# A 2x2 average pool on one Trainium2 core: one vector reduction per tile in place of two adds, and one store for two tiles

## Chip, cores, metric

One core of one Trainium2 chip. The metric is device time in microseconds (us) of the whole kernel. Executions of the kernel before agree within 0.02%. Each experiment ran together with the kernel before on one chip; where two experiments are compared with each other, the kernel before is the link, and its medians in all sets of runs lie between 3104.07 and 3104.31 us.

Names of the profile: DVE is VectorE, ACT is ScalarE, SP is the engine that issues the loads, ACTq and SPq are the sequencers that issue DMAs, L55 is line 55 of that kernel. "Span" is the time from the first to the last instruction of the profiled run, about 2 us under the device time.

## The reference

```python
# x: float32 [32, 128, 256, 256], kernel_size 2, stride 2
output[:, :, i, j] = np.mean(x[:, :, 2*i:2*i+2, 2*j:2*j+2], axis=(2, 3))
```

1073.74 MB are read and 268.44 MB written; three additions and a multiplication make one output.

## The kernel before

Two input rows of one plane (2 x 256 values, adjacent in memory) make one output row of 128. Such units are dealt out in tiles of 32 units for each of the 128 partitions: 64 KB of input and 16 KB of output per partition. There are 127 whole tiles; the last 32 units are loaded in parts of 16, 8, 4 and 4, so that little work is left after the last load.

```python
TILE = 32
in_pool  = tile_pool(bufs=2)      # 2 x 64 KB per partition
out_pool = tile_pool(bufs=4)      # 4 x 16 KB per partition

def pool(it, dst):
    nc.vector.tensor_add(out=it[:, :, 0:w], in0=it[:, :, 0:w], in1=it[:, :, w:])   # L54: the two rows
    nc.vector.tensor_add(out=dst, in0=it[:, :, 0:w:2], in1=it[:, :, 1:w:2])        # L55: the two columns
    nc.scalar.mul(out=dst, in_=dst, mul=0.25)                                      # L56

for k in range(whole):                          # 127 tiles
    it, res = tiles()
    nc.sync.dma_start(out=it, in_=xt)           # load
    pool(it, res)
    if k < whole - 1:
        nc.scalar.dma_start(out=ot, in_=res)    # store, 2 MB
    else:
        held = (ot, res)                        # its store is issued after the last loads
# ... the parts of the last 32 units are loaded; then the held store; then for each part:
    pool(it[:, a:b], res[:, a:b])
    nc.scalar.dma_start(out=ot, in_=res[:, a:b])
```

With two input buffers, the load of tile k+2 can be issued only when VectorE has finished with tile k.

## Time and profile before

| | before |
|---|---|
| device time, median | 3104.2 us (3104.09 to 3104.42) |
| DMA rate over the span | 433 GB/s |
| mean time from one tile's load landing to the next one's, in mid-run | 24.20 us |
| VectorE per whole tile | 8.69 + 4.43 us |

From the page of the kernel before: the instructions and shares of the engines, the DMA packets, the two DMA queues (q1 carries the loads, q10 the stores; the last number is the time that their packets took, as a share of 16 DMA engines over the span), the chain that ended last, and the DMA issues (how many, KB each where the page has it, median us from issue to landing).

```profile
span 3102.3 us, 1081 instructions
...
DVE 1679.7 (54%) x262; ACT 464.8 (15%) x132; POOL 0.2 (0%) x4
...
DMA packets 37736, 1342.26 MB, mean 433 GB/s; under 512 B 4192, under 2 KB 4192, under 8 KB 4576
...
q1 hardware_dynamic: 19008, 1075.85, 80.1%
q10 hardware_dynamic: 18720, 266.35, 20.1%
...
DMA 72%; DVE 27%; issue 0%; DVEq 0%; ACT 0%; SPq 0%
...
out_dram<-res ACTq DMA_DIRECT2D x126, 2048.0 KB, 31.6
...
in_tile<-in_x_dram SPq DMA_DIRECT2D x127, 35.1
```

The groups of instructions, forms apart, of the kernel before. After the bar: busy us in all, mean ns of one | idle time of the engine just before them, and what ended it.

```profile
L54 DVE TENSOR_TENSOR in_tile<-in_tile 128x8192 f32<-128x8192 f32 x127 | 1103.9, 8692 | 1402.8 <-DMA in_tile<-in_x_dram 1402.8
L55 DVE TENSOR_TENSOR res<-in_tile 128x4096 f32<-128x4096 f32 x127 | 562.1, 4426 | 11.7 <-DVE in_tile L54 0.5
```

The two queues add up to 100% of the 16 engines' time. That is the limit of this kernel: in the packet records a 64 KB packet of a load takes 2.418 us and a 16 KB packet of a store 0.611 us (medians), and a tile has 8 of each on every engine. VectorE idles 1402.8 us before the row adds of the whole tiles, every time for a load. The 27% of VectorE in the chain is no cost by itself: the chain follows one buffer at a time (load, adds, next load into that buffer), while the other buffer's load keeps the engines busy. A load takes 35.1 us from issue to landing, where the period is 24.2 us, because it is issued 10.9 us before the load ahead of it lands and queues behind that one. This time is called the lead below. While the DMA engines set the pace, it is about the period less VectorE's time on a tile: 24.2 - 13.2 us here.

The end of the kernel before, from its timeline (start us, us, engine, line, operation, [idle before <- what ended it]):

```profile
3067.22 8.69 DVE L54 TENSOR_TENSOR in_tile<-in_tile 128x8192 f32<-128x8192 f32 x1 [10.96 <-DMA in_tile<-in_x_dram]
3076.00 4.42 DVE L55 TENSOR_TENSOR res<-in_tile 128x4096 f32<-128x4096 f32 x1
...
3081.76 4.42 DVE L54 TENSOR_TENSOR in_tile<-in_tile 128x4096 f32<-128x4096 f32 x1 [1.34 <-DMA in_tile<-in_x_dram]
...
3086.28 2.29 DVE L55 TENSOR_TENSOR res<-in_tile 128x2048 f32<-128x2048 f32 x1
...
3093.81 1.22 DVE L54 TENSOR_TENSOR in_tile<-in_tile 128x1024 f32<-128x1024 f32 x1
...
3095.06 0.69 DVE L55 TENSOR_TENSOR res<-in_tile 128x512 f32<-128x512 f32 x1
...
3096.45 0.34 ACTq L94 DMA_DIRECT2D out_dram<-res  x1
```

The last whole tile's load lands at 3067.2 us. VectorE then works almost without a break on that tile and on the four parts until 3095.75 us, and the last small store lands 4.9 us after its issue.

### The profile page before, as it was taken

To read this page: it belongs to the slowest core of one execution; us is meant where nothing else is said; L and a number is where in the kernel's file an instruction comes from. 1 tells how busy PE (TensorE), PEld (TensorE's weight loads), DVE (VectorE), ACT (ScalarE), POOL (GpSimd) and SP (SyncE) were. 2 spreads that over 40 slices of the span, in tenths; PEclk is the share of its full clock that TensorE was granted. 3 is DMA by queue.
4 is the path that set the end of the run, shared out by engine and by line. 5 is a ranking of instruction groups with operands and counts; after the bars stand their busy time and mean duration, and the time that the engine had idled before them with its cause. 6 is when DMAs were issued, how large, how long until landed. Compare 5 with 4: busy or idle time off the path is not lost.

```text
span 3102.3 us, 1081 instructions
## 1 busy us (share of the span) xinstructions
DVE 1679.7 (54%) x262; ACT 464.8 (15%) x132; POOL 0.2 (0%) x4
## 2 busy tenths in 40 slices
DVE  4555555555555555555555555555555555555556
ACT  1111111111111111111111111111111111111111
POOL 0000000000000000000000000000000000000000
DMA  9999999999999999999999999999999999999999
GB/s 418 437 439 425 437 439 424 438 438 425 438 437 425 439 436 426 439 434 428 440 433 429 439 432 431 438 431 433 437 428 437 437 428 436 437 428 436 437 428 410
DMA packets 37736, 1342.26 MB, mean 433 GB/s; under 512 B 4192, under 2 KB 4192, under 8 KB 4576
## 3 DMA queue, kind: packets, MB, share of 16 engines
q1 hardware_dynamic: 19008, 1075.85, 80.1%
q10 hardware_dynamic: 18720, 266.35, 20.1%
q14 instruction: 8, 0.07, 0.0%
HBM read 1073.74 MB, written 268.44 MB: 433 GB/s over the span
## 4 chain that ended last, share of the span: by engine, by line
DMA 72%; DVE 27%; issue 0%; DVEq 0%; ACT 0%; SPq 0%
DMA in_tile<-in_x_dram 72%; DVE in_tile L54 18%; DVE res L55 9%; DVEq L55 0%; ACT res L56 0%; SPq L74 0%
## 5 line engine op out<-in xcount | busy, mean ns | idle before, releaser
L54 DVE TENSOR_TENSOR in_tile<-in_tile 128x8192 f32<-128x8192 f32 (+1 forms) x131 | 1113.0, 8496 | 1404.2 <-DMA in_tile<-in_x_dram 1404.2
L56 ACT ACTIVATE res<-res 128x4096 f32<-128x4096 f32 (+1 forms) x131 | 463.5, 3538 | 2630.9 <-DVE res L55 2630.9
L55 DVE TENSOR_TENSOR res<-in_tile 128x4096 f32<-128x4096 f32 (+1 forms) x131 | 567.0, 4328 | 11.8 <-DVE in_tile L54 0.5
L56 ACT ACT_TABLE_LOAD x1 | 1.3, 1283 | 0.7 <-PEq L171 0.7
L171 POOL MEMSET const-bfloat16-1.0<- 128x1 bf16 x1 | 0.1, 102 | 0.0
L171 POOL MEMSET const-uint8-127<- 128x1 uint8 x1 | 0.1, 101 | 0.0
L171 POOL MEMSET const-float32-0.0<- 128x1 f32 x1 | 0.1, 99 | 0.2 <-issue 0.2
L171 POOL MEMSET const-float32-1.0<- 128x1 f32 x1 | 0.1, 98 | 0.0
## 6 DMA issues: line engine op xcount, KB each, us to landing
out_dram<-res ACTq DMA_DIRECT2D x126, 2048.0 KB, 31.6
in_tile<-in_x_dram SPq DMA_DIRECT2D x1, 4096.0 KB, 25.5
in_tile<-in_x_dram SPq DMA_DIRECT2D x1, 2048.0 KB, 30.0
in_tile<-in_x_dram SPq DMA_DIRECT2D x2, 1024.0 KB, 33.0
out_dram<-res SPq DMA_DIRECT2D x1, 2048.0 KB, 13.6
in_tile<-in_x_dram SPq DMA_DIRECT2D x127, 35.1
out_dram<-res ACTq DMA_DIRECT2D x1, 1024.0 KB, 8.3
out_dram<-res ACTq DMA_DIRECT2D x1, 512.0 KB, 6.1
```

Source lines behind the costliest of these rows:

```text
L54: nc.vector.tensor_add(out=it[:, :, 0:w], in0=it[:, :, 0:w], in1=it[:, :, w:])
L55: nc.vector.tensor_add(out=dst, in0=it[:, :, 0:w:2], in1=it[:, :, 1:w:2])
L56: nc.scalar.mul(out=dst, in_=dst, mul=0.25)
L171: nc = _bacc.Bacc("TRN2", target_bir_lowering=False, num_devices=1)
```

## The change

The intent: one VectorE instruction per tile instead of two, and half as many stores, each twice as large. A `tensor_reduce` over the axes XY of a rearranged view sums the four values of an output. Two tiles share one output buffer of 2 x 16 KB per partition and one store of 4 MB; there are two such buffers, so four tiles fit as before, but their room comes free by pairs. The diff is shortened: the old loop and the new view `ot` of the output are left out.

```diff
-    out_pool = ctx.enter_context(tc.tile_pool(name="outp", bufs=4))
+    out_pool = ctx.enter_context(tc.tile_pool(name="outp", bufs=2))
-    def pool(it, dst):
-        nc.vector.tensor_add(out=it[:, :, 0:w], in0=it[:, :, 0:w], in1=it[:, :, w:])
-        nc.vector.tensor_add(out=dst, in0=it[:, :, 0:w:2], in1=it[:, :, 1:w:2])
-        nc.scalar.mul(out=dst, in_=dst, mul=0.25)
+    def sums(it, dst):
+        win = it.rearrange("p g (a j b) -> p g j a b", a=2, b=2)
+        nc.vector.tensor_reduce(out=dst, in_=win, axis=mybir.AxisListType.XY, op=mybir.AluOpType.add)
 # ... in the loop over whole tiles
+        if k % 2 == 0:
+            res = out_pool.tile([P, 2, TILE, w_out], f32, name="res")
+        sums(it, res[:, k % 2])
+        nc.scalar.mul(out=res[:, k % 2], in_=res[:, k % 2], mul=0.25)
+        if k % 2 == 1 or k == whole - 1:
+            n = k % 2 + 1
+            store = ot[:, k + 1 - n:k + 1], res[:, 0:n].rearrange("p t g f -> p t (g f)")
+            if k < whole - 1:
+                nc.scalar.dma_start(out=store[0], in_=store[1])
 # ... the last 32 units
+    last = out_pool.tile([P, 2, TILE, w_out], f32, name="res")
+    for to, a, b in parts:
+        dst = last[:, 0, a:b]
+        sums(it[:, a:b], dst)
+        nc.scalar.mul(out=dst, in_=dst, mul=0.25)
+        nc.scalar.dma_start(out=to, in_=dst)
```

More of the change, by code (lines that the diff above doesn't have):

```diff
@@ L61, in block @@
         return xt, ov[rows].rearrange("(p g) f -> p g f", p=P)
-    def tiles():
-        it = in_pool.tile([P, TILE, 2 * w], f32, name="in_tile")
-        return it, out_pool.tile([P, TILE, w_out], f32, name="res")
     whole, rest = divmod(units - 1, TILE)
     rest += 1
+    ot = ov[0:whole * TILE * P].rearrange("(t p g) f -> p t (g f)", p=P, g=TILE)
     for k in range(whole):
-        xt, ot = block(k * TILE * P, TILE)
-        it, res = tiles()
-        nc.sync.dma_start(out=it, in_=xt)
-        pool(it, res)
-        if k < whole - 1:
-            nc.scalar.dma_start(out=ot, in_=res)
-        else:
-            held = (ot, res)
-    it, res = tiles()
+        it = in_pool.tile([P, TILE, 2 * w], f32, name="in_tile")
+        nc.sync.dma_start(out=it, in_=block(k * TILE * P, TILE)[0])
+        if k % 2 == 0:
[7 more added lines that the diff above has]
+                nc.scalar.dma_start(out=store[0], in_=store[1])
+    it = in_pool.tile([P, TILE, 2 * w], f32, name="in_tile")
+    last = out_pool.tile([P, 2, TILE, w_out], f32, name="res")
     parts, a = [], 0
@@ L86, in _pool_2x2 @@
         b = rest if rest - a <= 4 else a + (rest - a) // 2
-        xt, ot = block((whole * TILE + a) * P, b - a)
+        xt, to = block((whole * TILE + a) * P, b - a)
         nc.sync.dma_start(out=it[:, a:b], in_=xt)
-        parts.append((ot, a, b))
+        parts.append((to, a, b))
         a = b
-    nc.sync.dma_start(out=held[0], in_=held[1])
-    for ot, a, b in parts:
-        pool(it[:, a:b], res[:, a:b])
-        nc.scalar.dma_start(out=ot, in_=res[:, a:b])
+    nc.sync.dma_start(out=store[0], in_=store[1])
+    for to, a, b in parts:
[3 more added lines that the diff above has]
+        nc.scalar.dma_start(out=to, in_=dst)
 def _generic_pool(ctx, tc, x, out, k, s, n, c, h, w, h_out, w_out):
```

## The prediction

> **What bounds the kernel now.** The 16 DMA engines. The queue table gives the loads 80.1% and the stores 20.1% of 16 engines' span: nothing is left. In the packet records a 64 KB load packet takes 2.418 us and a 16 KB store packet 0.611 us (medians), both about 27 GB/s per engine. The Trainium skill ("DMA: Bandwidth & Descriptors", Specifications) puts the ceiling of the 16 engines at 435 GB/s; the page of this trace has 433. A tile period is 24.2 us (8 load packets and 8 store packets per engine, 8 x 3.03 us). VectorE is 54% busy: per tile 8.69 us (rows) and 4.43 us (columns), then 11 us waiting for the load (waits view). The chain of waits reads DMA 72%, DVE 27%, but DVE there costs nothing: a load takes 35.1 us from issue to landing against a period of 24.2 us, so while VectorE frees one buffer the other load keeps the engines busy.
>
> **What the change does.** No byte is saved. Two adds (13.1 us, 12288 outputs per partition) become one reduction that reads 16384. The adds fit (elements + about 150) / 0.96 ns; the Trainium skill ("VectorE: DVE Perf Modes", The perf-mode tier table) gives tensor_reduce only 1x, one element per cycle. Estimate: 16384 elements at the traced slope of 1.04 ns = 17.2 us per tile. No trace shows a reduction yet. VectorE then goes from 54% to about 71% busy: 4 us more per tile, off the critical path while busy time plus waiting stays under 24.2 us. 126 stores become 63 of 4 MB with the same packets.
>
> **New wait.** The output buffer holds four tiles as before, but comes free by pairs. If the queues alternate packet by packet, as a store's 31.6 us for 8 packets suggests (8 x 3.03 = 24.2 us, plus the rest of the store before it), a pair's 16 packets need 48.4 us and land about 55 us after issue. Issued 20.8 us after the second tile's load, it lands some 76 us after that; the next tile to need the buffer arrives after three periods (72.6 us). So VectorE should wait about 3 to 4 us for the store at every second tile, 200 us in total, inside its slack (17.2 + 3.6 < 24.2).
>
> **Where it shows in the time.** Only at the end. After the last full tile's load VectorE needs 13.1 + 15.3 us now; then 17.2 + 17.7 us, plus several us waiting until the pair before frees the third buffer. About 15 us are added there, of which some 5 to 7 come back because deferred stores let that load land earlier. Net +8 us (estimate).
>
> **Prediction: 3112 us, range 3103 to 3130. Faster by over 2%: 0.01; within 2%: 0.91; slower by over 2%: 0.08.**
>
> **What would show it.** Right: a reduction near 17.2 us; VectorE about 70% busy; queue shares still adding to 99 to 100%, about 432 GB/s; a wait of VectorE for the store of res, 3 to 4 us at every second tile; pair store about 55 us to landing, loads about 30; the last full load landing earlier than 3067 us, but the end later. Wrong step by step: reduction of 22 us or more (windows of four cost extra cycles); no wait for the store (queues don't alternate as I think).
>
> **What would make it wrong.** The reduction costing extra per window or per jump between rows: above about 23.5 us it sets the period, and each further us per tile costs 128 us (26 us: about 3350). Pair stores whose packets are split unevenly over the engines, or starving the loads.

## The result and the profile after

The median went from 3104.31 to 3110.51 us (3110.2 to 3110.88, 4 runs of each). The ratio is 1.002, 95% interval 1.0005 to 1.0035. Ratios are the mean time of one kernel's fast runs over that of the other's of the same rounds, so not quite the ratio of the medians quoted.

From the page of the changed kernel, the lines that answer to those above:

```profile
span 3108.4 us, 824 instructions
...
DVE 2204.3 (71%) x131; ACT 464.8 (15%) x132; POOL 0.2 (0%) x4
...
DMA packets 36727, 1342.25 MB, mean 432 GB/s; under 512 B 3184, under 2 KB 3184, under 8 KB 3568
...
q1 hardware_dynamic: 19008, 1075.85, 79.9%
q10 hardware_dynamic: 17712, 266.34, 20.0%
...
DMA 64%; DVE 35%; DVEq 0%; ACT 0%; issue 0%; SPq 0%
...
out_dram<-res ACTq DMA_DIRECT2D x63, 4096.0 KB, 51.6
...
in_tile<-in_x_dram SPq DMA_DIRECT2D x127, 31.0
```

Its groups of instructions, forms apart:

```profile
L55 DVE TENSOR_REDUCE res<-in_tile 128x4096 f32<-128x16384 f32 x127 | 2186.9, 17220 | 893.4 <-DMA in_tile<-in_x_dram 885.0 <-DMA out_dram<-res 8.4
...
L55 DVE TENSOR_REDUCE res<-in_tile 128x2048 f32<-128x8192 f32 x1 | 8.7, 8686 | 7.1 <-DMA out_dram<-res 7.1
```

Both kernels over the same stretch of mid-run, 1000 to 2000 us (busy time of the engines, granted clock, share of the DMA engines, GB/s); first the kernel before, then the changed one:

```profile
1000.00:2000.00 1000.00, 537.83 (x82) 151.07 (x42) 0.00 (x0) 1.00 1.00 433
```
```profile
1000.00:2000.00 1000.00, 707.75 (x43) 151.88 (x42) 0.00 (x0) 1.00 1.00 434
```

In mid-run nothing was lost: VectorE has 170 us more to do in 1000 us, the DMA engines are at 1.00 in both, and the period is 24.18 us against 24.20. What is new is at the end. The timeline of the changed kernel there:

```profile
3063.12 17.22 DVE L55 TENSOR_REDUCE res<-in_tile 128x4096 f32<-128x16384 f32 x1 [7.24 <-DMA in_tile<-in_x_dram]
...
3087.43 17.40 DVE L55 TENSOR_REDUCE res<-in_tile 128x2048 f32<-128x8192 f32 x4 [7.09 <-DMA out_dram<-res]
...
3105.52 0.34 ACTq L95 DMA_DIRECT2D out_dram<-res  x1
```

The account from this timeline and the one shown of before, in us:

| | before | after | difference |
|---|---|---|---|
| VectorE starts on the last whole tile | 3067.22 | 3063.12 | -4.1 |
| VectorE on that tile (to 3080.42; 3080.34) | 13.20 | 17.22 | +4.0 |
| wait until the first part can start | 1.34 | 7.09 | +5.8 |
| the four parts | 13.99 | 17.40 | +3.4 |
| from there to the end of the span | 6.55 | 3.59 | -3.0 |
| span | 3102.3 | 3108.4 | +6.1 |

The last whole tile's load lands earlier because some store traffic has been put off behind it: with the pair store alone (e2 below) it lands at 3062.0 us, with the reduction alone (e1) at 3067.0. The wait of 7.09 us is for the pair store of tiles 124 and 125, whose buffer the parts need. The last stores no longer queue behind others: the very last lands 2.0 us after issue, before it was 4.9 us.

### The profile page after: what moved, and what is told of

The parts are those of the page before. It is cut to its first block, busy times and chain, and to the rows that moved or that the text cites. A ratio compares the mean times of both kernels' runs of the same rounds, so it can differ in the third digit from the quotient of the medians.

```text
span 3108.4 us, 824 instructions
## 1 busy us (share of the span) xinstructions
DVE 2204.3 (71%) x131; ACT 464.8 (15%) x132; POOL 0.2 (0%) x4
## 4 chain that ended last, share of the span: by engine, by line
DMA 64%; DVE 35%; DVEq 0%; ACT 0%; issue 0%; SPq 0%
DMA in_tile<-in_x_dram 63%; DVE res L55 35%; DMA out_dram<-res 1%; DVEq L186 0%; ACT res L72 0%; ACT res L94 0%; SPq L68 0%; DVEq L55 0%
## 5 line engine op out<-in xcount | busy, mean ns | idle before, releaser
L55 DVE TENSOR_REDUCE res<-in_tile 128x4096 f32<-128x16384 f32 (+1 forms) x131 | 2204.3, 16829 | 900.5 <-DMA in_tile<-in_x_dram 885.0
L72 ACT ACTIVATE res<-res 128x4096 f32<-128x4096 f32 x127 | 459.2, 3616 | 2622.7 <-DVE res L55 2622.7
## 6 DMA issues: line engine op xcount, KB each, us to landing
out_dram<-res ACTq DMA_DIRECT2D x63, 4096.0 KB, 51.6
```

Source lines behind the costliest of these rows:

```text
L55: nc.vector.tensor_reduce(out=dst, in_=win, axis=mybir.AxisListType.XY, op=mybir.AluOpType.add)
L72: nc.scalar.mul(out=res[:, k % 2], in_=res[:, k % 2], mul=0.25)
```

## Experiments

The theory: mid-run is bound by the DMA engines and does not change; the +6 us are made after the last whole tile's load, by a slower VectorE and by the wait for a pair store. Rivals: the reduction slows the DMA stream; or the pair store makes the whole cost. Twelve kernels ran, all with correct results.

### Each half alone

e1_reduce_only is the kernel before with the reduction:

```diff
-        nc.vector.tensor_add(out=it[:, :, 0:w], in0=it[:, :, 0:w], in1=it[:, :, w:])
-        nc.vector.tensor_add(out=dst, in0=it[:, :, 0:w:2], in1=it[:, :, 1:w:2])
+        win = it.rearrange("p g (a j b) -> p g j a b", a=2, b=2)
+        nc.vector.tensor_reduce(out=dst, in_=win, axis=mybir.AxisListType.XY, op=mybir.AluOpType.add)
```

> Edit: the kernel before with its two adds replaced by the one reduction; stores stay single, four output buffers. Theory (all of the cost lies after the last full tile's load; in mid-run the DMA engines set the pace): the last full load lands where it did in the kernel before (3067 us of the span), then VectorE needs 17.2 + 17.4 us in place of 13.1 + 15.3, ends about 6 us later, and about 3 us come back because the last small stores no longer queue behind others: time +3 us on the kernel before, so 3106 to 3109, no wait of VectorE for a store. Rival A (the pair store makes the whole cost): 3104 to 3105. Rival B (the reduction slows the DMA stream in mid-run, e.g. by SBUF contention): the mean period of a tile rises over 24.20 us and the whole +6 us shows here.

Measured: 3107.36 us (3107.01 to 3108.84) against 3104.07 us of before (3103.98 to 3104.43); ratio 1.0011, interval 0.9999 to 1.0024. The difference of 3.3 us is small against the interval of the ratio, but the ranges of the runs don't touch. Mean period in mid-run 24.18 us, so rival B falls. The last whole tile's load lands at 3067.0 us as before, VectorE works from there on without a break and ends at 3101.6 us, 5.8 us later than before, and never waits for a store:

```profile
3067.04 34.53 DVE L55 TENSOR_REDUCE res<-in_tile 128x4096 f32<-128x16384 f32 x5 [6.96 <-DMA in_tile<-in_x_dram]
```

e2_pair_only is the changed kernel with the two adds:

```diff
-        win = it.rearrange("p g (a j b) -> p g j a b", a=2, b=2)
-        nc.vector.tensor_reduce(out=dst, in_=win, axis=mybir.AxisListType.XY, op=mybir.AluOpType.add)
+        nc.vector.tensor_add(out=it[:, :, 0:w], in0=it[:, :, 0:w], in1=it[:, :, w:])
+        nc.vector.tensor_add(out=dst, in0=it[:, :, 0:w:2], in1=it[:, :, 1:w:2])
```

> Edit: the changed kernel with the two adds put back; pair stores stay. Theory: the last full load lands near 3063 us (stores are put off), VectorE ends that tile at 3076, then waits for the pair store of tiles 124 and 125 to free the third buffer until about 3083 to 3085, then 13.5 us of parts and 3 to 4 us of last store: 3101 to 3104 of span, so time 3102 to 3106, about 0 to +2 on the kernel before, with one wait of VectorE for a store of 7 to 9 us at the end. Rival A (pair store makes the cost): 3110.

Measured: 3104.10 us (3103.89 to 3104.48), ratio 1.0, interval 0.9987 to 1.0014. Rival A falls: the pair store alone costs nothing. The wait at the end is there, but 2.9 us long and not 7 to 9, because the row add of the first part needs no output buffer and runs while the store is still landing (waits from 3000 us to the end):

```profile
DVE res L55 <- DMA out_dram<-res: 2.9, 1, 2.9
```

The halves alone give +3.3 and 0.0 us, both together +6.2. So about 2.9 us come only from the two together: with the reduction the first part's only instruction needs the buffer at once.

### The wait at the end

e3_free_half takes the wait away from the changed kernel. Tile 126 has no partner, so half of its output buffer is unused, and the parts go there:

```diff
-    last = out_pool.tile([P, 2, TILE, w_out], f32, name="res")
-        dst = last[:, 0, a:b]
+        dst = res[:, 1, a:b]
```

> Edit: the changed kernel, but the last small parts are written into the unused second half of tile 126's output buffer, so that they wait for no earlier store. Theory: the last wait of 7 us goes; parts run at once after tile 126 (3080 us), the last ends near 3098, span about 3101 to 3103, time 3103 to 3106: 5 to 7 us below the changed kernel. Rival C (the last wait is slack, since the last loads land only at 3092 and DMA work ends when it ends): unchanged, 3110.

Measured: 3105.29 us (3104.54 to 3105.83), 5.2 us under the 3110.51 us of the changed kernel. The waits of the changed kernel, then of this one, from 3000 us to the end (who waited for whom: us in total, times, longest):

```profile
DVE res L55 <- DMA in_tile<-in_x_dram: 27.8, 4, 7.2
...
DVE res L55 <- DMA out_dram<-res: 7.1, 1, 7.1
```
```profile
DVE res L55 <- DMA in_tile<-in_x_dram: 27.9, 4, 7.2
ACT res L94 <- DVE res L55: 10.1, 4, 5.0
```

The second list has no wait for out_dram. So the 7.1 us wait was on the path, and rival C falls. The rest of the +6 us, about 1 us, is what the slower VectorE still costs: e4 below, which differs from this run in the two adds alone, is 1.3 us faster.

e4_adds_free_half has the two adds, pair stores and the free half together (the edits of the last two runs).

> Edit: the pair-store kernel with the two adds (as in the run before the last) and the last parts in the free half. Theory: VectorE done with each part about 2 us after its load lands (3092), span 3098 to 3101, time 3100 to 3103, one to four us below the kernel before: the most that this schedule can give, since the DMA engines are then busy nearly to the end. Rival: no better than the kernel before, 3104.

Measured: 3103.97 us (3103.94 to 3104.07), ratio 1.0. My expectation of 3100 to 3103 was missed, and the rival holds. VectorE does end a little earlier, at 3094.6 us, but the last load lands at 3092.6 us and the put-off stores are still in the queue, so that the last store takes 6.1 us to land. With the bytes given, no version of these parts beats the kernel before by anything that the runs can tell.

### Does a store wait for the one before it?

I had predicted a wait of VectorE for a store at every second tile, 200 us in all. The changed kernel has two waits that a store ended in the whole run: 8.4 us at the fifth tile, of which only the last 0.8 us are the store's (that tile's load had landed by then), and 7.1 us at the end. A pair store took 51.6 us to land, not 55, and landed 0.18 us before the load of the tile that needs its buffer (the median from the sixth pair on; the least is 0.18 too). I thought that 55 us failed because the backlog of stores, which I had read off the kernel before, is made once at the start. e5_single_two tests it with single stores in two output buffers:

```diff
 # e1_reduce_only, and
-    out_pool = ctx.enter_context(tc.tile_pool(name="outp", bufs=4))
+    out_pool = ctx.enter_context(tc.tile_pool(name="outp", bufs=2))
```

> Edit: single stores and the one reduction, with two output buffers of one tile in place of four. A store is issued 20.8 us after its tile's load landed, and the buffer is needed again 48.4 us after that landing, so only 27.6 us are there for a store; in the kernel before a store took 31.6 us. View 1 (the step of the prediction that failed: the queue keeps a standing backlog from store to store): VectorE waits about 4 us for a store at every tile, some 500 us in all, still hidden (17.2 + 4 < 24.2), time 3107 to 3111. View 2 (the backlog is made at the start only, where the first two loads land 19.3 us apart while a store takes 24.2 us, and a wait drains it for good): one to three waits at the start, under 15 us in all, stores then land in 27.2 to 27.6 us, time 3107 to 3111 as well. The waits view tells the two apart, not the time.

Measured: 3186.40 us (3177.23 to 3197.19), ratio 1.0276, interval 1.0247 to 1.0306. Neither view had this: both expected at most 3111 us. The waits of this run:

```profile
DVE res L55 <- DMA out_dram<-res: 942.7, 125, 13.9
DVE res L55 <- DMA in_tile<-in_x_dram: 24.8, 2, 22.7
```

VectorE waits 7.5 us in the mean for a store, at 125 of 127 tiles. The time closes over one buffer: a store is issued 20.9 us after VectorE starts on its tile and lands 28.5 us later, 49.4 us for two tiles, 24.7 us each. So a wait at every tile (view 1), but not hidden. At the same time packets became longer: with the engines busy all the time, a load's packet took 2.481 us in the mean of mid-run, not 2.418, and 8 of them with 8 of a store (0.611 us) fill 24.7 us as well. Which of the two comes first, the late store or the long packets, this run can't tell. The long packets were new, and the next runs meet them again.

### How much slack does VectorE have?

The prediction held that VectorE is free up to the period of 24.2 us. e6_pad4 and e7_pad9 add work to the changed kernel that nobody needs, and that holds the input buffer longer:

```diff
         sums(it, res[:, k % 2])
+        nc.vector.tensor_add(out=it[:, 0:16, 0:w], in0=it[:, 0:16, 0:w], in1=it[:, 0:16, w:])   # e6: 4.4 us
+        nc.vector.tensor_add(out=it[:, :, 0:w], in0=it[:, :, 0:w], in1=it[:, :, w:])            # e7 instead: 8.7 us
```

> Edit: the changed kernel plus one add of 4096 outputs (4.4 us) on the input tile after every full tile's reduction: work that nobody needs, which holds the input buffer 4.4 us longer. VectorE 21.7 us per tile. Theory (slack of 24.2 us per tile): mean period of a tile stays 24.18 us within 0.05; at the end the extra 4.4 us falls into the 7 us wait for the pair store, so the time stays 3109 to 3113. Rival (VectorE time costs in mid-run, its 35% of the chain of waits being real): a part of 127 x 4.4 = 560 us shows, at least 3160.

Measured: 3353.86 us (3353.42 to 3354.91), ratio 1.0805. My theory falls. The rival's range holds, but its reason does not survive e9 and e10 below: they add 127 x 2.3 and 127 x 1.2 us to VectorE and cost 8.0 and 1.3 us. Mid-run of this run and its DMA queues, to be held against those above:

```profile
q1 hardware_dynamic: 19008, 1075.85, 75.1%
q10 hardware_dynamic: 17712, 266.34, 20.1%
```
```profile
1000.00:2000.00 1000.00, 827.08 (x79) 141.08 (x39) 0.00 (x0) 1.00 0.95 400
```
```profile
1506.86 17.22 DVE L55 TENSOR_REDUCE res<-in_tile 128x4096 f32<-128x16384 f32 x1 [8.98 <-DMA in_tile<-in_x_dram]
...
1524.11 4.42 DVE L72 TENSOR_TENSOR in_tile<-in_tile 128x4096 f32<-128x4096 f32 x1
1527.76 0.38 ACTq L78 DMA_DIRECT2D out_dram<-res  x1
1528.46 17.21 DVE L55 TENSOR_REDUCE res<-in_tile 128x4096 f32<-128x16384 f32 x1
...
1545.70 4.42 DVE L72 TENSOR_TENSOR in_tile<-in_tile 128x4096 f32<-128x4096 f32 x1
1559.16 17.22 DVE L55 TENSOR_REDUCE res<-in_tile 128x4096 f32<-128x16384 f32 x1 [9.04 <-DMA in_tile<-in_x_dram]
```

VectorE takes two tiles without a break, then idles 9.0 us: 52.3 us for two tiles. The DMA engines are at 0.95 here. The packet records show why. The load queue runs dry at 1526.4 us, because VectorE frees the next buffer only at 1528.5 us. That load is issued 0.8 us after a pair store. Its first packet starts 5.0 us after its issue, and until then the pair store has the engines to itself, 7 of its 16 packets per engine. The stores are then over early, the other load of the pair runs without stores in 19.7 us, and the queue runs dry again. The rhythm repeats to the end: landings are 32.3 and 19.9 us apart in turn.

> Edit: the same with an add of 8192 outputs (8.7 us). VectorE 25.96 us per tile with its gaps, over the 24.2 us that the DMA engines need. Theory: VectorE now sets the period, 25.96 us; 22.95 + 127 x 25.96 = 3320 us at the end of the last full tile, then 17.4 us of parts and about 6 us: 3335 to 3350, VectorE 99% busy, about 402 GB/s. If the slack were less than I think, more; if the DMA engines could give way, less.

Measured: 3397.52 us (3396.45 to 3398.44), ratio 1.0945. VectorE is 97% busy and all but sets the period, but the time is 48 us above my range: VectorE waits 0.9 to 1.0 us at every second tile, 62 us in all, as a late load takes 26.9 us to land. So of the 287 us that 8.7 us per tile cost (against 3110.51), 243 had come with the first 4.4 us.

### Is it the start, the lead or the pair?

e8_pad4_late adds the 4.4 us only from the ninth tile on, when the regular rhythm stands:

```diff
         sums(it, res[:, k % 2])
+        if k >= 8:
+            nc.vector.tensor_add(out=it[:, 0:16, 0:w], in0=it[:, 0:16, 0:w], in1=it[:, 0:16, w:])
```

> Asked because the run with 4.4 us more per tile took 250 us more, where I had expected none. Edit: the same extra add of 4.4 us, but only from the ninth tile on, so that the start is that of the changed kernel. View S (the start decides: while no store was in flight a load took 19.3 us, VectorE's 21.7 us let the load queue run dry, and the bad rhythm then repeats; once stores are queued without a gap a load takes 24.2 us and 21.7 us fit): 3110 to 3116. View L (lead decides: in the changed kernel a load is issued 6.9 us before the one ahead of it lands; with 4.4 us less, and a load that is issued just after a pair store giving its first packet only 5 us later, the load queue runs dry at once, stores go alone, and the later load runs without stores at 19.3 us): 3340 to 3356, land-to-land times alternating near 32 and 20 us.

Measured: 3334.97 us (3332.70 to 3337.02), ratio 1.0743. The range of view L began 5 us higher, but view S is out by 219 us: the good rhythm holds for two tiles after the work is added, and then it falls into the bad one (32.3 and 19.9 us). The first gap shows how: load 10 is issued when the load ahead has 1.2 us of packets left, and its first packet starts 3.6 us after the issue. The last pair store had been issued 25.3 us earlier and was still landing.

e9_pad2 and e10_pad1 add 2.3 and 1.2 us (`it[:, 0:8, ...]` and `it[:, 0:4, ...]` in the line of e6).

> Edit: the changed kernel plus an add of 2048 outputs (2.3 us) per full tile, VectorE 19.55 us per tile, lead 4.6 us. It lies just over the 19.3 us that a load takes with no store in flight and just under the 5 us of a load's first packet behind a pair store. View L and S: beginning of the loss, 3115 to 3250. View of a slack of 24.2 us (already damaged): 3109 to 3113.

> Edit: the same with an add of 1024 outputs (1.2 us), VectorE 18.5 us per tile, lead 5.6 us. Both views: still no loss in mid-run, mean period 24.18 us, time 3109 to 3114. If 3130 or more, the changed kernel itself stands at the edge of its slack.

Measured: e9 3118.47 us (3116.98 to 3121.27), e10 3111.80 us (3111.42 to 3112.09). Both keep the regular rhythm, with 434 GB/s in mid-run (e9 below); the profiled run of e9, the slowest of its four, has lost some 9 us by the last whole tile. With pair stores the edge lies between 19.5 and 21.7 us of VectorE per tile.

```profile
1000.00:2000.00 1000.00, 804.13 (x84) 151.90 (x42) 0.00 (x0) 1.00 1.00 434
```

e11_pad4_single is e1_reduce_only with the 4.4 us added after each whole tile's pooling:

```diff
         pool(it, res)
+        nc.vector.tensor_add(out=it[:, 0:16, 0:w], in0=it[:, 0:16, 0:w], in1=it[:, 0:16, w:])
```

> Edit: the same extra add of 4.4 us in every full tile, but in the kernel with the reduction and single stores (four output buffers): what the pair store does to the slack. If the loss comes from stores going out by pairs and running alone while a late load makes its first packet: 3108 to 3170, far below 3354. If it is the time of VectorE against the loads alone, whatever the stores: 3340 to 3356 as with pairs.

Measured: 3194.16 us (3174.15 to 3199.45), ratio 1.0278. It is above my range of 3170 at the median, yet 160 us below the pair stores with the same VectorE time. The loss is there without pairs (87 us on e1), and larger with them (243 us on the changed kernel).

e12_pad4_first turns the order of issue round:

```diff
+        nc.vector.tensor_add(out=res, in0=it[:, :, 0:w_out], in1=it[:, :, w_out:w])   # overwritten by the sums
         pool(it, res)
```

> Edit: as the run before (reduction, single stores, 4.4 us more of VectorE per full tile, result right), but the extra add comes ahead of the reduction and writes the output buffer that the reduction then overwrites. VectorE time per tile and the load's lead over the one ahead of it are those of that run; only the order of issue turns round: each load is now issued 3.7 us before the tile's store, where it was issued 0.8 us behind it. View P (a load's first packet is late because a store was issued just before it): 3108 to 3130. View Q (any store in flight makes a load's first packet come 2 to 5 us after its issue, so a lead under 3 us lets the load queue run dry whatever the order): 3160 to 3220, as in the run before (3194).

Measured: 3230.03 us (3227.55 to 3233.26), ratio 1.0403. The time that view P expected is far off; the measured one is 10 us above the range of view Q, and Q's reason falls as well: here the first packet starts 1.0 to 2.4 us after the issue (median 1.7), while the load ahead still has packets, and there is no gap. In e11 the same delay was 3.4 to 4.6 us, so the order of issue, the difference that was meant between the two, seems to change it. But a store issued just before is not needed for a late first packet: in e8 it came 3.6 us after the issue with the last store issued 25.3 us earlier, and in e7 4.9 us with the store issued 5.1 us earlier, against 0.95 us for the other loads of that run, issued with no store in flight. What sets the delay stays open. The mid-run of this run:

```profile
1000.00:2000.00 1000.00, 860.20 (x80) 144.48 (x40) 0.00 (x0) 1.00 1.00 417
```

The engines are never idle, yet move 417 GB/s: a load's packet takes 2.537 us in the mean. Eight packets at 0.119 us more are 0.95 us per tile, and the measured period is 25.2 us against 24.2. So the loss shows in two ways: a DMA share under 1 (0.95 in e6) and longer packets (e12). An add on VectorE does not by itself make packets long: the kernel before has two in every tile, and its load packets take 2.418 us.

The runs that bear on the slack, side by side. The lead is how long before the landing of the load ahead a load is issued, the mean of mid-run from issue and landing times; the packet is the mean of the 64 KB load packets from 1000 to 2000 us; the DMA share and rate are the windows view of that stretch.

| kernel | VectorE per tile, us | lead, us | load packet, us | DMA share, GB/s | time, us |
|---|---|---|---|---|---|
| before | 13.1 | 10.9 | 2.418 | 1.00, 433 | 3104.2 |
| changed | 17.2 | 6.9 | 2.418 | 1.00, 434 | 3110.5 |
| e1, single stores | 17.2 | 6.8 | 2.418 | 1.00, 434 | 3107.4 |
| e10, +1.2 | 18.5 | 5.6 | 2.418 | 1.00, 434 | 3111.8 |
| e9, +2.3 | 19.5 | 4.6 | 2.420 | 1.00, 434 | 3118.5 |
| e5, waits for stores | 17.2 + 7.5 wait | 4.4 | 2.481 | 1.00, 425 | 3186.4 |
| e6, +4.4, pairs | 21.7 | 3.6 (9.0 and -1.8 in turn) | 2.453 | 0.95, 400 | 3353.9 |
| e12, +4.4 first, single | 21.7 | 3.3 | 2.537 | 1.00, 417 | 3230.0 |
| e11, +4.4, single | 21.7 | 3.1 | 2.460 | 1.00, 421 | 3194.2 |
| e8, as e6 from the ninth tile | 21.7 | 3.5 (8.9 and -1.8 in turn) | 2.447 | 0.95, 402 | 3335.0 |
| e7, +8.7, pairs | 25.9 | -2.1 (0.9 and -5.1 in turn) | 2.489 | 0.96, 397 | 3397.5 |

In these runs the DMA rate holds down to a lead of 4.6 us and is lost below. e5 speaks for the lead and against VectorE's own time: VectorE works 17.2 us per tile as in the changed kernel, and the rate is lost all the same. But e5 also differs in its stores, and no run gave the lead back at an unchanged time of VectorE, so the lead as the cause is argued and not shown. Why packets lengthen then, I did not find; it stays open. The packet records do show where: of the 8 packets of a load on each engine, in e12 the third and fourth take 2.69 and 2.72 us in the mean of 40 loads and the last three 2.44 to 2.46; in e6 it is the first packet of the load behind the pair store, 2.95 us.

## Why the prediction was right, and where it was not

- **The bound: right.** "The 16 DMA engines", with no byte saved. Mid-run has 433 and 434 GB/s, periods 24.20 and 24.18 us.
- **The reduction: right.** 17.2 us was the estimate, from the Trainium skill ("VectorE: DVE Perf Modes", The perf-mode tier table), which gives tensor_reduce only the 1x mode, and from the slope of the traced adds. The trace agrees with one element per 1.04 ns: 17220 ns for 16384 elements. Windows of four and jumps between two rows cost nothing extra.
- **"Only at the end": right, shown by e1 to e3.** The forecast was 15 us added and 5 to 7 given back, net +8. Measured in the trace: 13.2 us added, 4.1 given back by the earlier load and 3.0 by the faster last stores, net +6.1 of span, +6.2 of time. The 3.0 us were not in the forecast; that the sum came so near is in part luck.
- **The wait at every second tile: wrong.** The failed term is "plus the rest of the store before it", about 7 us that I took over from the kernel before; it measured 51.6 - 48.4 = 3.2 us. A pair store landed after 51.6 us, 3.4 less than predicted. That is enough to land 0.18 us before the load that VectorE needs anyway, so no wait shows. The miss cost nothing, but the margin is hardly there. Why the rest is 3.2 us and not 7 was not settled: e5 was meant to, and fell outside both views. The prediction's own reading of a missing wait, "queues don't alternate as I think", is not what happened (last point).
- **"Off the critical path while busy time plus waiting stays under 24.2 us": wrong, and it stayed hidden in the result.** The step compared VectorE's time with the period, and took it that a freed buffer is filled at once. e6 has VectorE at 21.7 us and loses 243 us on the changed kernel; e5 has a wait that should have hidden and loses 79 us on e1. The failed step is that all of the period could be spent: in these runs some 5 us of lead had to be left over (kept at 4.6 us in e9, lost at 4.4 us in e5). The change used up 4.1 us of a lead of 10.9 and stands at 6.9, above that edge. Likewise "above about 23.5 us it sets the period" was too high by 2 to 4 us.
- **The alternation of queues: right for the regular rhythm only.** The Trainium skill ("DMA: Bandwidth & Descriptors", Queues, rings and completion order) says that each engine takes packets from its queues in turn. The trace of the changed kernel agrees: in the median stretch of 3.03 us of mid-run 16 load packets and 16 store packets start. But where one queue is empty for a moment (e6), the other takes all, and the stores are used up before the loads.

## What to carry to other kernels

This kernel, with full DMA queues, gained nothing from fewer instructions or fewer, larger stores; look instead at what runs after the last whole load, where added compute and waits for a buffer are no longer hidden behind loads. (Not all of it counts: in e4 VectorE ended earlier, and the last store still landed at 3101.4 us, as in the kernel before.) The slack of the compute engine in a double-buffered loop is not all of the period less its busy time: see how long before the landing of the load ahead the next load is issued, and keep several microseconds there. A result of "same" does not show how much slack is left; adding useless work in steps does.

## What the Trainium skill lacked or had wrong

- "DMA: Bandwidth & Descriptors", Latency and other measured facts, gives about 600 ns to the first byte of such a DMA. With nothing in flight the first load's first packet starts 1.0 us after the start of the issuing instruction and 0.6 us after its end, which fits. With stores in flight and the load queue running empty, 3.6 us (e8) to 5.0 us (e6) from the start were seen. I found no page that has this.
- I found no page that says that packets get longer when a load is issued late: 2.418 us for 64 KB with a lead of 5.6 us or more, 2.537 us at 3.3 us (e12), with the engines busy all the time.
- "DMA: Bandwidth & Descriptors", Where 436 GB/s comes from, says, without a condition, that about 358 GB/s bind for transfers between HBM and SBUF. This one core moved 433 GB/s over a whole kernel, reads and writes together, near the 435 GB/s of the same page's Specifications. The section just before it on that page, with its measured table (425 GB/s for a core alone), ties the 358 to both cores of an HBM pair streaming, which fits.
- "VectorE: DVE Perf Modes", The perf-mode tier table, has no time for tensor_reduce. Here it is 17.220 us for 16384 fp32 elements in windows of 2 x 2, and 2.275 us for 2048; two adds of the same tile take 8.692 + 4.426 us.
